# A decoder layer on one core: convolution taps of token tiles 3 and 4 issued behind the second output projection, with a pause, and one norm's rows in other buffers

## The chip, the cores and the metric

One NeuronCore of one Trainium2 chip runs the whole layer as one program. The metric is the device time of one execution in microseconds (us). TensorE (PE) multiplies, VectorE (DVE) and ScalarE (ACT) do the elementwise work, GpSimd (POOL) helps a little, and SyncE (SP) issues most DMAs. Each engine takes its own instructions in the order in which they stand in the program.

## The reference, cut to what matters

```python
hn = rms_norm(h, mix_pre_g); proj = hn @ w_in              # q, k, v and the GLU input u
attn_out = sliding_window_attention(q, k, v, ...)          # window 128, 8 heads
conv_out = conformer_conv(u, ...)                          # GLU, depthwise conv of width 31, LayerNorm, swish, pointwise
mixed = concatenate([attn_out, conv_out]) @ w_out
h = h + rms_norm(mixed, mix_post_g)
hn = rms_norm(h, ffn_pre_g)
ff = (silu(hn @ w_gate) * (hn @ w_up)) @ w_down            # 1024 -> 2816 -> 1024
h = h + rms_norm(ff, ffn_post_g)
```

There are 2048 tokens of width 1024, in float32. Every product is made of three matmuls on a high and a low part of both operands, so each weight and each activation is split first: ACT makes the high part, DVE subtracts it and so makes the low part.

## The kernel before, in words

The 2048 tokens stand in four tiles of 512, numbered 0 to 3 in the code (tile "3 and 4" of the change's name are 2 and 3, "tile 2" is 1). A letter and a number name a stage in every tile's name: A0 to A3 are the input projections, B0 to B3 attention, C0 to C3 the convolution, J0 the joining of two weights, W0 to W3 the output projection with its two norms, H0 and H2 the operands of the feed-forward part for the tile pairs (0, 1) and (2, 3), F0 and F2 its gate and up products for these pairs, G0 and G2 its down products.

A main chain of generators runs in this order: A0 to A3, W1, the first products of F0 (`stage_pre`, 40 products of 12 matmuls with the operands B11 and B21 of tile 0), the rest of F0 (`stage_p1`, whose products need sums over both tiles, made by `stage_h_sums`, called S0), G0, then F2 and G2. Beside it run "lanes". After each step of the main chain each lane is given credit in proportion to the step's length and to its own rate, and issues work until the credit is used (`Lane.pump`). A lane whose `hold()` is true issues nothing. A scheduler then places the instructions of each engine by priority; the lane `lc` has a lag of 100, so that its work stands behind what the main chain issues about then.

`lc` holds the convolution taps: T0, T1 for tiles 0 and 1, T2 for tiles 2 and 3 together. T2 has four channel blocks. For each, `conv_in` loads 527 KB into g2, the first tap is a TENSOR_SCALAR, and 30 taps follow, each a SCALAR_TENSOR_TENSOR of 128x1024 on DVE (line 622 through the recorder on line 85). Then y2 is stored to y_scr. g2 and y2 have one buffer each, so the next block's load and first tap follow that store. T2 runs at rate RC2 = 0.35, and from the third last weight block of F0 at RC3 = 0.9. From the end of W1's main part on, `lc.hold` keeps the taps back until S0 is done.

W1 accumulates into four `mid` tiles. Its second part, `norm_w`, runs in the lane `lh` as N1: it squares the rows (ACT, line 857), takes a first reciprocal root, scales, adds the residual rows of x (loaded by line 870 and 876), stores h, squares again (line 879), takes a second reciprocal root of 12 small DVE instructions (sm@W), scales the four tiles (line 886, ACT) and stores them to hn_scr. The residual rows of its second row block load into two buffers of the tag `mtag`. For W1 that is "at", which has two buffers and is also where attention puts its outputs until they are stored to mixT.

S0 then loads hn_scr back by columns (line 900), turns the blocks on PE (line 922) and makes, for each of four k, five sums on DVE and four splits (ACT and DVE each) in the buffers "chl", of which there are five. F0's second part uses the same five for the loads of its weights' lower halves and for their sums S1 to S4 (`loads`, `sums`), and splits them three products ahead (`split`).

W2, W3, then H2's first half and N3 (the norm of W3) stand in the lane `lw` and run beside G0. W2 and W3 may start only when T2 is done (`since(lc, "T2", CS)`).

Of the kernel before, what the change touches and what calls it, by code (L numbers as in the profile page):

```python
# [37 lines left out]
def layer_kernel(ctx, tc, x, xT, cols, rows, sinks, relb, onehot, w_in, w_four, w_pw, w_out, w_gate, w_up, w_down, out):  # L38
# [16 lines left out]
    def t_(tag, shape, dt=F32):  # L55
        return sb.tile(list(shape), dt, tag=tag, name=nm(tag), bufs=BUFS[tag])

    def f4(tag, shape=(P, D)):
        return t_(tag, shape)

    def f2(tag, shape=(P, T)):
        return t_(tag, shape)

    def hl(tag):
        return t_(tag, (P, 2, T), F32R)

    def sm(n, dt=F32):
        kind = "A" if lab[0][0] == "G" else lab[0][0]
        return sb.tile([P, 8], dt, tag="sm" + kind, name=nm("sm"), bufs={"C": 8, "W": 4}.get(kind, 16))[:, 0:n]

    def bank(tag, bufs):
        return ps.tile([P, T], F32, tag=tag, name=nm(tag), bufs=bufs)

    mm = lambda: bank("mm", 4)
# [178 lines left out]
    y_scr = dr.tile([4, P, S], F32, name="y_scr")  # L253
    qs = {}
    started = set()

    def load_x(t):
        lab[0] = f"A{t}"
        xs = []
        for i in range(4):  # L260
            xt = f4("x", (P, 2, T))
            nc.sync.dma_start(xt, xT[2 * i : 2 * i + 2, :, t * T : (t + 1) * T].rearrange("c p t -> p c t"))
            xs.append(xt)
        started.add(f"x{t}")
        return [xs]
# [368 lines left out]
    def stage_tail(t, sink=None):  # L634
        L = f"C{t}"
        lab[0] = L
        yt = t_("yt", (P, 4, 4 * P))
        ycs = []
        turn = turner(yt, ycs)
        for c in range(4):  # L640
            lab[0] = L
            y = f2("fc")
            nc.sync.dma_start(y, y_scr[c, :, t * T : (t + 1) * T])
            ycs.append(y)
            turn(c)
            yield 0.5
        yield from conv_tail(t, yt, sink)
# [34 lines left out]
    def spare_tile():  # L682
        if not spare:
            spare.append(t_("mb", (P, 2, T)))
        return spare[0]
# [89 lines left out]
    def load_gb(row):  # L775
        gb = []
        for n in range(2):
            t = f2("gb")
            nc.sync.dma_start(t, rows[row, n * T : (n + 1) * T].partition_broadcast(P))
            gb.append(t)  # L780
        return gb
# [6 lines left out]
    def stage_w(w, spill, G, atag, htag, mtag, bank_of, norm=None):  # L788
        L = f"W{w}"
        lab[0] = L  # L790
        acc = [f4(atag) for _ in range(4)]

        def operand(m):
            a = hl(htag)
            act(a[:, 0], m, AF.Copy)
            vtt(a[:, 1], m, a[:, 0].bitcast(F32), ALU.subtract)
            return [a]

        def acts(gi, ms=None):
            return [operand(m) for m in ms or load(gi)]  # L800

        conv = []
        tail = stage_tail(w, lambda v: conv.append(operand(v))) if w > 1 else ()
        for y in tail:
            if y == YL2:
                break
            yield y
        lab[0] = L

        stage = spare_tile() if w == 1 else None  # L810

        def load(gi):
            ms = []
            pair_ = stage if w == 1 else t_("chl", (P, 2, T)) if w else t_("wx", (P, 2, T)) if gi == 0 else None
            for c in range(G * gi, G * gi + G):
                ms.append(pair_[:, c % 2] if pair_ is not None else f2(mtag))
                nc.sync.dma_start(ms[-1], mixT[c, :, w * T : (w + 1) * T])
            return ms

        first = load(0)  # L820
        gb = load_gb(0) if w > 1 else None
        if w != 1:
            yield 5.0 if w == 0 else 8.0
            lab[0] = L
        nxt = acts(0, first)
        for gi in range(KC // G):
            if w > 1 and G * gi == 4:
                yield from tail
                lab[0] = L
            aa = nxt if w < 2 or G * gi < 4 else conv[G * gi - 4 : G * gi - 4 + G]  # L830
            for n in range(2):
                lab[0] = L
                more = gi + 1 < KC // G and (w < 2 or G * gi + G < 4)
                if n == 0 and more:
                    if w < 2 and G * gi + G == 4:
                        ld.until(f"C{w}")
                        lab[0] = L
                    rows_next = load(gi + 1)
                if n == 1 and more:
                    nxt = acts(gi + 1, rows_next)  # L840
                src = w_out[2 * gi : 2 * gi + 2] if gi < 2 else w_join[2 * gi - 4 : 2 * gi - 2]
                ws = weight(src[:, :, n * T : (n + 1) * T].rearrange("c p t -> p c t"),
                            lo_out[n, 2 * gi : 2 * gi + 2], w > 0, on_pool=False)
                yield from block_half(acc, list(zip(aa, ws)), n, gi == 0, L, bank_of)
        last = norm_w(w, spill, acc, mtag, gb)
        if norm:
            norm(last)
        else:
            yield from last

    def norm_w(w, spill, acc, mtag, gb):
        L = f"W{w}"
        lab[0] = L
        gb = gb or load_gb(0)
        ssq = sm(4)
        for s in range(4):
            act(junk, acc[s], AF.Square, accum_out=ssq[:, s : s + 1])
            yield 0.5
            lab[0] = L
        r = rsqrt(ssq, 4, D, False)  # L860
        yield 3
        lab[0] = L
        ssq2 = sm(4)
        for s in range(4):
            lab[0] = L
            post_scale(acc[s], gb, r[:, s : s + 1])
            r0 = w * T + s * P
            if s == (2 if mtag == "fa" else 0):
                xt = f4("wx")
                nc.sync.dma_start(xt, x[r0 : r0 + P])  # L870
                vtt(acc[s], xt, acc[s], ALU.add)
            else:
                for n in range(2):
                    cs = slice(n * T, (n + 1) * T)
                    xt = f2(mtag if s == 1 or w > 1 else "fa")
                    nc.sync.dma_start(xt, x[r0 : r0 + P, cs])
                    vtt(acc[s][:, cs], xt, acc[s][:, cs], ALU.add)
            nc.sync.dma_start(h_scr[r0 : r0 + P], acc[s])
            act(junk, acc[s], AF.Square, accum_out=ssq2[:, s : s + 1])
            yield 5.0  # L880
        lab[0] = L
        r2 = rsqrt(ssq2, 4, D, False)
        yield 3
        lab[0] = L
        for s in range(4):
            act(acc[s], acc[s], AF.Copy, scale=r2[:, s : s + 1])
        if spill:
            yield 2.0
            lab[0] = L
            for s in range(4):  # L890
                r0 = w * T + s * P
                nc.sync.dma_start(hn_scr[r0 : r0 + P], acc[s])
        yield 0.1
        hns[w] = acc
# [301 lines left out]
    def stage_tsums(td):  # L1196
        L = "G0"
        for pr in range(NF // 2):
            lab[0] = L
            wx = f4("wx", (P, 2, T))  # L1200
            b = [wx[:, 0], wx[:, 1], f2("fc"), f2("fc")]
            for i, (f, n) in enumerate(((0, 0), (0, 1), (1, 0), (1, 1))):
                tied(nc.sync.dma_start(b[i], w_down[2 * pr + f, :, n * T : (n + 1) * T]))
            yield 5
            b11, b12, b21, b22 = b
            for to, o, p_, q_ in ((0, b11, b12, b11), (2, b12, b22, b12), (1, b22, b22, b11), (3, b21, b21, b22)):
                lab[0] = L
                vtt(o, p_, q_, ALU.subtract)
                nc.sync.dma_start(td[to, pr], o)
                yield 1  # L1210
# [244 lines left out]
    RC0, RC1, RC2, RC3, RW0, RW, RB, LC = 0.7, 1.1, 0.35, 0.9, 1.7, 1.25, 0.8, 100  # L1455
# [13 lines left out]
    PRE_S0, PRE_S2 = 22, 16  # L1469
# [5 lines left out]
    lc = Lane(RC0, LC)  # L1475
    lw = Lane(RW0, 0)
    lf = Lane(1.2, 0)
    lh = Lane(1.2, 0)
# [7 lines left out]
    def run(gen):  # L1486
        for c in gen:
            clk[0] += c
            for lane in lanes:
                lane.pump(c)  # L1490
# [62 lines left out]
    ws, ops = (0, 1), {}  # L1553
    for n, off in (("B11", 0), ("B21", 4)):
        lh.add(n + ".0", stage_h_plain(ws, ops, n, off), lambda: since(lw, "W0", NH))
    run(stage_w(1, True, 2, "mid", "hl", "at", mm, norm=lambda g: lh.add("N1", g)))
    lc.hold = lambda: "S0" not in lh.done
    lh.add("S0", stage_h_sums(ws, ops), lambda: f"P0.{PRE_S0}" in started and "B3" in lb.done)
    run(stage_pre(ws, ops, mids[0], keeps[0]))
    lt.add("TS", stage_tsums(td))  # L1560
    run(stage_p1(ws, ops, mids[0], keeps[0]))
    lt.until("TS")
    ws, ops = (2, 3), {}
# [76 lines left out]
```

## Time and profile before

| | us |
|---|---|
| three runs | 1906.05, 1906.81, 1908.97 |
| median | 1906.81 |
| profiled execution, span from first to last instruction | 1907.9 |

The profiled execution lies within the three runs, 1.1 us above their median. Its span is what all windows and waits below are counted in, from 0 at the first instruction.

F0's first product starts at 517.84 us, the first product on S0's operands at 639.50 us, F2's first product at 1265.49 us. A matmul's record has a modelled end and overlaps the next one, so how fast PE goes is read from the distance between starts. A row of the list of waits gives who waited, for whom, the total, the count and the longest. A row of the timeline gives start, length, engine, line, operation, written and read tiles, size and count, and in brackets the engine's idle time before it with what ended it.

### The profile page before, as it was taken

To read this page: it belongs to the slowest core of one execution; us is meant where nothing else is said; L and a number is where in the kernel's file an instruction comes from. 1 tells how busy PE (TensorE), PEld (TensorE's weight loads), DVE (VectorE), ACT (ScalarE), POOL (GpSimd) and SP (SyncE) were. 2 spreads that over 40 slices of the span, in tenths; PEclk is the share of its full clock that TensorE was granted. 3 is DMA by queue.
4 is the path that set the end of the run, shared out by engine and by line. 5 is a ranking of instruction groups with operands and counts; after the bars stand their busy time and mean duration, and the time that the engine had idled before them with its cause. 6 is when DMAs were issued, how large, how long until landed. Compare 5 with 4: busy or idle time off the path is not lost.

```text
span 1907.9 us, 26569 instructions
## 1 busy us (share of the span) xinstructions
PE 1889.1 (99%) x8714; PEld 1530.1 (80%) x8714; DVE 1490.7 (78%) x2721; ACT 970.6 (51%) x1912; POOL 179.2 (9%) x196
## 2 busy tenths in 40 slices
PE   9999999999999999999999999999999999999998
PEld 8777777777777888888888878788888888888886
DVE  6999999987966999999996765887567674455558
ACT  5356445566667433433445574685443433345452
POOL 2010001110000000000000000010033233211002
PEclk9999999999999999999999999999999999999999
DMA  9887746679688677877776596798554443375663
GB/s 353 300 281 238 248 160 207 230 228 318 218 274 276 232 234 232 293 261 243 244 268 195 196 326 212 259 333 307 166 176 156 160 138 127 116 258 187 206 220 133
DMA packets 226491, 439.29 MB, mean 230 GB/s; under 512 B 22536, under 2 KB 48560, under 8 KB 226352
## 3 DMA queue, kind: packets, MB, share of 16 engines
q1 hardware_dynamic: 207344, 411.37, 64.8%
q10 hardware_dynamic: 17088, 19.93, 2.9%
q0 software_dynamic: 1920, 6.29, 0.9%
q8 instruction: 68, 1.11, 0.2%
q14 instruction: 71, 0.58, 0.1%
HBM read 318.48 MB, written 119.02 MB: 229 GB/s over the span
## 4 chain that ended last, share of the span: by engine, by line
PE 78%; DVE 9%; DMA 8%; ACT 3%; issue 2%; SPq 0%; ACTq 0%; DVEq 0%; POOL 0%; POOLq 0%
PE mm@F L108 34%; PE mm@G L108 16%; PE mm@A L108 14%; PE tr@W L108 5%; PE mm@W L108 3%; PE tr@B L108 2%; PE ct@J L108 1%; DVE w@F L85 1%; DVE mid@W L85 1%; DMA hl@A<-x 1%; DVE sm@G L85 1%; DVE y2@C L85 1%; DMA chl@H<-hT 1%; DVE hl@G L85 1%; DMA chl@F<-w_gate 1%
## 5 line engine op out<-in xcount | busy, mean ns | idle before, releaser
L108 PE MATMUL mm@F<-hl@H,w@F 128*128 128x512 f32 x1056 | 255.8, 391 | 1.8 <-ACT mm@F L1058 1.6
L108 PEld LDWEIGHTS mm@F<-hl@H,w@F 128*128 128x128 f32 x1056 | 197.7, 188 | 44.8 <-ACT mm@F L1058 2.8
L108 PE MATMUL mm@G<-hl@G,hl@G 128*128 128x512 f32 x924 | 226.1, 393 | 2.3 <-ACT hl@G L904 1.5
L904 ACT ACTIVATE w@F<-chl@F 128x512 fp32r<-128x512 f32 x220 | 136.5, 626 | 170.2 <-PE mm@F L108 158.7
L108 PEld LDWEIGHTS mm@G<-hl@G,hl@G 128*128 128x128 f32 x924 | 171.5, 188 | 39.7 <-ACT hl@G L904 2.2
L108 PE MATMUL mm@G<-w@G,hl@G 128*128 128x512 f32 x876 | 199.8, 389 | 0.6 <-DVE w@G L85 0.6
L108 PEld LDWEIGHTS mm@G<-w@G,hl@G 128*128 128x128 f32 x876 | 164.3, 188 | 35.2 <-DVE w@G L85 1.0
L108 PE MATMUL mm@A<-hl@A,w@A 128*128 128x512 f32 x792 | 192.2, 394 | 0.0
L108 PEld LDWEIGHTS mm@A<-hl@A,w@A 128*128 128x128 f32 x792 | 146.8, 188 | 32.5 <-issue 1.7
L85 DVE TENSOR_TENSOR w@F<-chl@F,w@F 128x512 fp32r<-128x512 f32 x198 | 148.1, 753 | 25.5 <-ACT w@F L904 25.0
L85 DVE SCALAR_TENSOR_TENSOR y2@C<-g2@C,colt,y2@C 128x1024 f32<-128x1024 f32 x120 | 154.0, 1283 | 0.2
L108 PE MATMUL mm@F<-mid@H,w@F 128*128 128x512 f32 x528 | 130.6, 390 | 1.0 <-DVE w@F L85 0.9
L108 PE MATMUL mm@F<-ql@H,w@F 128*128 128x512 f32 x528 | 129.7, 390 | 0.2
L108 PE MATMUL mm@F<-p@H,w@F 128*128 128x512 f32 x528 | 129.1, 389 | 0.0
L108 PE MATMUL mm@F<-x@H,w@F 128*128 128x512 f32 x528 | 127.8, 390 | 0.0
L108 PEld LDWEIGHTS mm@F<-mid@H,w@F 128*128 128x128 f32 x528 | 98.8, 188 | 22.2 <-DVE w@F L85 1.3
L108 PEld LDWEIGHTS mm@F<-ql@H,w@F 128*128 128x128 f32 x528 | 98.7, 188 | 21.3 <-DVE w@F L85 0.6
L108 PEld LDWEIGHTS mm@F<-x@H,w@F 128*128 128x128 f32 x528 | 98.7, 188 | 21.3 <-issue 0.8
L108 PEld LDWEIGHTS mm@F<-p@H,w@F 128*128 128x128 f32 x528 | 99.1, 188 | 20.6
L133 ACT ACTIVATE w@A<-raw@A 128x512 fp32r<-128x512 f32 x100 | 60.9, 625 | 80.2 <-PE mm@A L108 46.3
L85 DVE TENSOR_TENSOR w@G<-raw@G,w@G 128x512 fp32r<-128x512 f32 x72 | 50.2, 698 | 64.2 <-ACT w@G L904 63.4
L108 PE MATMUL mm@W<-w@W,hl@W 128*128 128x512 f32 x384 | 97.1, 399 | 0.8 <-DVE x@W L85 0.4
(322 smaller groups left out, 3363.9 us busy)
## 6 DMA issues: line engine op xcount, KB each, us to landing
mids<-fa@F SPq DMA_DIRECT2D x154, 256.0 KB, 3.3
raw@A<-w_in SPq DMA_DIRECT2D x50, 512.0 KB, 4.9
w@A<-lo_in SPq DMA_DIRECT2D x84, 256.0 KB, 4.0
fa@G<-mids SPq DMA_DIRECT2D x74, 256.0 KB, 4.7
fc@G<-mids SPq DMA_DIRECT2D x72, 256.0 KB, 3.5
w@W<-lo_out SPq DMA_DIRECT2D x48, 256.0 KB, 4.8
chl@F<-w_gate SPq DMA_DIRECT2D x22, 512.0 KB, 4.4
raw@F<-w_gate SPq DMA_DIRECT2D x22, 512.0 KB, 4.2
```

What stands on the lines that cost most here:

```text
L85: r = op(*args, **kw)
L108: r = nc.tensor.matmul(*args, **kw)
L133: act(w[:, 0], raw, AF.Copy)
L904: act(w[:, 0], x, AF.Copy)
```

## The change

```diff
@@ -253,6 +253,7 @@
     started = set()
+    flags = set()
@@ -877,10 +878,13 @@
             act(junk, acc[s], AF.Square, accum_out=ssq2[:, s : s + 1])
+            if s == 2:
+                flags.add("root")
             yield 5.0
         lab[0] = L
         r2 = rsqrt(ssq2, 4, D, False)
         yield 3
+        flags.discard("root")
         lab[0] = L
@@ -1553,11 +1557,13 @@
-    run(stage_w(1, True, 2, "mid", "hl", "at", mm, norm=lambda g: lh.add("N1", g)))
-    lc.hold = lambda: "S0" not in lh.done
+    run(stage_w(1, True, 2, "mid", "hl", "fc", mm, norm=lambda g: lh.add("N1", g)))
+    lc.rates["T2"] = RC3
+    lc.hold = lambda: "root" in flags or f"P0.{PRE_S0}" in started and "S0" not in lh.done
     lh.add("S0", stage_h_sums(ws, ops), lambda: f"P0.{PRE_S0}" in started and "B3" in lb.done)
     run(stage_pre(ws, ops, mids[0], keeps[0]))
     lt.add("TS", stage_tsums(td))
+    lc.rates["T2"] = RC2
     run(stage_p1(ws, ops, mids[0], keeps[0]))
```

The taps of T2 are no longer held from W1's main part on: they run at rate 0.9 in `stage_pre`, are held while N1 is at its second root, and are held again from the 23rd product of `stage_pre` (PRE_S0 = 22) until S0 is done. In `stage_p1` the rate is 0.35 again. The two residual row loads of N1 go to "fc" buffers, which the convolution's tail used before. No instruction is added or removed. What moves is shown at three places, the third on two engines.

**DVE at the second root of N1.** sm@W1 are the root's small instructions, w@F0 the low parts of F0's weights, y2@C2 the taps. Before:

```order
L85 TENSOR_TENSOR mid@W1_787_4738<-at@W1_980_5673,mid@W1_787_4738 128x512
L85 TENSOR_TENSOR w@F0_1028_5984<-raw@F0_1025_5950,w@F0_1028_5984 128x512
L85 TENSOR_TENSOR w@F0_1033_6008<-raw@F0_1029_5987,w@F0_1033_6008 128x512
L85 TENSOR_SCALAR sm@W1_998_5780<-sm@W1_963_5591 128x4
L85 TENSOR_SCALAR sm@W1_999_5781<-sm@W1_998_5780 128x4
L85 TENSOR_SCALAR sm@W1_999_5781<-sm@W1_999_5781 128x4
L85 TENSOR_TENSOR sm@W1_1000_5782<-sm@W1_999_5781 128x4
```

In the changed program:

```order
L85 TENSOR_TENSOR w@F0_1013_5880<-raw@F0_1005_5830,w@F0_1013_5880 128x512
L85 TENSOR_SCALAR y2@C2_958_5570<-g2@C2_957_5568,colt_73 128x1024
L85 TENSOR_SCALAR sm@W1_1000_5791<-sm@W1_965_5597 128x4
L85 SCALAR_TENSOR_TENSOR y2@C2_958_5570<-g2@C2_957_5568,colt_73,y2@C2_958_5570 128x1024
L85 TENSOR_SCALAR sm@W1_1001_5792<-sm@W1_1000_5791 128x4
L85 TENSOR_TENSOR w@F0_1016_5902<-raw@F0_1014_5883,w@F0_1016_5902 128x512
L85 SCALAR_TENSOR_TENSOR y2@C2_958_5570<-g2@C2_957_5568,colt_73,y2@C2_958_5570 128x1024
L85 TENSOR_SCALAR sm@W1_1001_5792<-sm@W1_1001_5792 128x4
L85 TENSOR_TENSOR w@F0_1017_5921<-raw@F0_1014_5883,w@F0_1017_5921 128x512
```

Before, the root starts behind the 21st w@F0 and its 12 instructions end behind the 23rd; now it starts behind the 14th and ends behind the 21st, with 11 full taps among its instructions.

**DVE where F0's second part begins.** chl@H0, ql@H0 and p@H0 belong to the last k of S0, the TENSOR_TENSOR chl@F0<-chl@F0 without raw is the sum S1 of a weight block, w@F0<-chl@F0 the splits that PE needs. Before, around the split w@F0_1173 of the second block:

```order
L85 TENSOR_TENSOR w@F0_1168_6677<-chl@F0_1153_6627,w@F0_1168_6677 128x512
L85 SCALAR_TENSOR_TENSOR y2@C2_1141_6548<-g2@C2_1140_6546,colt_73,y2@C2_1141_6548 128x1024
L85 TENSOR_TENSOR fa@F0_1151_6607<-fa@F0_1151_6607,mm@F0_1149_6590 128x512
L85 TENSOR_TENSOR chl@F0_1191_6815<-chl@F0_1180_6766 128x512
L85 TENSOR_TENSOR w@F0_1173_6705<-chl@F0_1170_6694,w@F0_1173_6705 128x512
```

In the changed program, from the end of S0 on:

```order
L85 SCALAR_TENSOR_TENSOR y2@C2_958_5570<-g2@C2_957_5568,colt_73,y2@C2_958_5570 128x1024
L85 TENSOR_TENSOR chl@F0_1156_6673<-chl@F0_1155_6671 128x512
L85 TENSOR_TENSOR chl@H0_1125_6485<-chl@H0_1119_6468,chl@H0_1125_6485 128x512
L85 TENSOR_TENSOR ql@H0_1137_6542<-chl@H0_1125_6485,ql@H0_1137_6542 128x512
L85 TENSOR_TENSOR fa@F0_1141_6566<-fa@F0_1141_6566,mm@F0_1135_6537 128x512
L85 TENSOR_TENSOR p@H0_1138_6545<-chl@H0_1124_6484,p@H0_1138_6545 128x512
L85 TENSOR_TENSOR chl@F0_1156_6673<-chl@F0_1156_6673,raw@F0_1154_6669 128x512
L85 TENSOR_TENSOR chl@F0_1157_6676<-raw@F0_1154_6669,chl@F0_1155_6671 128x512
L85 TENSOR_TENSOR w@F0_1158_6679<-chl@F0_1156_6673,w@F0_1158_6679 128x512
L85 TENSOR_TENSOR mid@H0_1142_6568<-chl@H0_1125_6485,mid@H0_1142_6568 128x512
L85 TENSOR_TENSOR chl@F0_1157_6676<-raw@F0_1154_6669,chl@F0_1156_6673 128x512
L85 TENSOR_SCALAR y2@C2_1049_6128<-g2@C2_1048_6126,colt_73 128x1024
```

Before, the sum of the third block (chl@F0_1191) stands directly ahead of the split w@F0_1173. In the changed program the splits of the first block stand among the last rows of S0 instead of behind them, a new channel block's first tap (y2@C2_1049) follows, and the third block's sum has gone behind the split that it preceded. By the first split of F0's second part 61 taps have been issued instead of 31; by G0's first split 124, which is all, instead of 100.

**PE at the end of G0.** tr@H2 are the turned blocks of N3's rows, the last operands of F2, mm@F2 its first products, mm@G0 the last ones of G0. Before:

```order
L108 MATMUL mm@G0_1547_9291<-hl@G0_2089_12171,hl@G0_2090_12174 128x512
L108 MATMUL mm@F2_2106_12277<-ql@H2_1930_11256,w@F2_2101_12262 128x512 x3
L108 MATMUL mm@F2_2106_12277<-ql@H2_1937_11283,w@F2_2101_12262 128x512 x3
L108 MATMUL mm@F2_2106_12277<-ql@H2_1941_11302,w@F2_2101_12262 128x512 x3
L108 MATMUL mm@F2_2106_12277<-ql@H2_1951_11340,w@F2_2101_12262 128x512 x3
L922 MATMUL tr@H2_2185_12716<-ident_68,fc@H2_2184_12714 128x128 x4
L922 MATMUL tr@H2_2187_12723<-ident_68,at@H2_2186_12721 128x128 x4
```

In the changed program:

```order
L108 MATMUL mm@G0_1546_9290<-hl@G0_2056_11962,hl@G0_2057_11965 128x512
L926 MATMUL tr@H2_2185_12716<-ident_68,fc@H2_2184_12714 128x128 x4
L108 MATMUL mm@G0_1547_9291<-hl@G0_2043_11875,hl@G0_2044_11878 128x512 x3
L108 MATMUL mm@G0_1547_9291<-hl@G0_2047_11898,hl@G0_2048_11901 128x512 x3
L108 MATMUL mm@G0_1547_9291<-hl@G0_2056_11962,hl@G0_2057_11965 128x512
L926 MATMUL tr@H2_2187_12723<-ident_68,at@H2_2186_12721 128x128 x4
```

Of the turned blocks of N3's rows the first now stand behind 813 and 820 of G0's 924 matmuls instead of behind all of them. W3's last matmul followed 660 of them before and follows 521 now.

**SP late in G0.** fa@G0 and mb@G0 are the loads of G0's products, hn_scr the four stores of the tiles that N3 has scaled on ACT. Before:

```order
L1262 DMA fa@G0_2078_12106<-mids0_4730 128x512
L1266 DMA mb@G0_2079_12108<-w_down 128x512 x2
L1262 DMA fa@G0_2082_12129<-mids0_4730 128x512
L1262 DMA fa@G0_2085_12149<-mids0_4730 128x512
L1266 DMA mb@G0_2086_12151<-w_down 128x512
L892 DMA hn_scr_125<-mid@W3_1762_10404 128x1024
L892 DMA hn_scr_125<-mid@W3_1763_10405 128x1024
```

In the changed program:

```order
L1266 DMA fa@G0_2038_11850<-mids0_4730 128x512
L896 DMA hn_scr_125<-mid@W3_1762_10404 128x1024
L896 DMA hn_scr_125<-mid@W3_1763_10405 128x1024
L896 DMA hn_scr_125<-mid@W3_1764_10406 128x1024
L896 DMA hn_scr_125<-mid@W3_1765_10407 128x1024
L1266 DMA fa@G0_2042_11873<-mids0_4730 128x512
L1270 DMA mb@G0_2039_11852<-w_down 128x512 x2
L1266 DMA fa@G0_2045_11893<-mids0_4730 128x512
L1270 DMA mb@G0_2046_11895<-w_down 128x512 x2
L1266 DMA fa@G0_2055_11960<-mids0_4730 128x512
L904 DMA fc@H2_2184_12714<-hn_scr_125 128x4x128
L904 DMA at@H2_2186_12721<-hn_scr_125 128x4x128
```

The four stores stood behind the loads of all of G0's products; now fa@G0_2042, mb@G0_2039 and what follows stand behind them, and these belong to the products at G0's 793rd to 829th matmul. On ACT the four scales stood behind the splits hl@G0_2081 (877th matmul) and stand behind hl@G0_2030 (745th) now.

## The prediction

> **What bounds the kernel now.** I read the page first, then the list of waits of PE from the start of F0's second part on, then the chain.
>
> ```profile
> span 1907.9 us, 26569 instructions
> PE 1889.1 (99%) x8714; PEld 1530.1 (80%) x8714; DVE 1490.7 (78%) x2721; ACT 970.6 (51%) x1912; POOL 179.2 (9%) x196
> ```
>
> PE is busy for 99% of the span, DVE for 78%. The change neither adds nor removes an instruction, so it can gain only what PE waits for, and lose only by new waits. The waits of PE between 565 us and the end, which holds everything that the change moves:
>
> ```profile
> PE mm@F L108 <- ACT mm@F L1058: 1.6, 1, 1.6
> PE mm@G L108 <- ACT hl@G L904: 1.5, 2, 0.8
> PE mm@F L108 <- DVE w@F L85: 0.9, 1, 0.9
> PE tr@H L922 <- DMA at@H<-hn_scr: 0.7, 1, 0.7
> PE mm@G L108 <- DVE p@G L1297: 0.6, 1, 0.6
> PE mm@G L108 <- DVE w@G L85: 0.6, 1, 0.6
> PE mm@F L108 <- DVE gb@F L85: 0.5, 1, 0.5
> PE mm@F L108 <- ACT gb@F L1159: 0.2, 1, 0.2
> ```
>
> All but the wait for w@G, which falls in G2, stand between the root of N1 and the first products of F2: 1.6 + 1.5 + 0.9 + 0.7 + 0.6 + 0.5 + 0.2 = **6.0 us**. That is the ceiling of the gain. From there on the chain says that PE has nothing to wait for:
>
> ```profile
> 1225.59 5.72 DMA mb@G<-w_down
> ...
> 1256.45 6.18 DMA hn_scr<-mid@W
> 1263.07 6.64 DMA at@H<-hn_scr
> ...
> 1295.02 391.70 PE mm@F L108 x1728
> ```
>
> **The taps and their room on DVE.** The 120 full taps and four first ones, by stretch, and the busy time of DVE in three stretches:
>
> ```profile
> L85 DVE SCALAR_TENSOR_TENSOR y2@C<-g2@C,colt,y2@C 128x1024 f32<-128x1024 f32 x120 | 154.0, 1283 | 0.2
> 482.00:543.00 61.00, 10.41 (x8) 1.00 0.63 215
> 543.00:634.00 91.00, 0.00 (x0) 1.00 0.83 279
> 634.00:951.00 317.00, 88.15 (x70) 1.00 0.75 248
> 951.00:1012.00 61.00, 29.43 (x23) 1.00 0.79 269
> ```
>
> ```profile
> 551.00:594.00 43.00, 14.96 (x32) 1.00 0.86 296
> 594.00:634.00 40.00, 36.75 (x59) 1.00 0.77 252
> 640.00:700.00 60.00, 54.18 (x78) 1.00 0.69 230
> ```
>
> The first four of these rows' windows count taps alone (busy us, then their number), the last three all of DVE. No tap runs from 543 to 634 us, and the last 23 of them run in G0. The order has 61 taps instead of 31 ahead of the first split of F0's second part, so 30 move into that gap. A tap takes 1283 ns by its group, and two that follow each other start about 1.20 us apart (the tap below at 646.34 is followed by the next start at 647.54). So the 30 need 30 x 1.20 = **36.0 us**. The room is 43.0 - 14.96 = 28.0 and 40.0 - 36.75 = 3.3, so **31.3 us**. At least 4.7 us do not fit and stand ahead of the work that follows. Between 640 and 700 another 60.0 - 54.18 = 5.8 us are idle, which can take that backlog up, though only once PE's first operands are past it.
>
> **Step 1, the root of N1.** The rows that carry it:
>
> ```profile
> 558.52 0.42 SPq L876 DMA_DIRECT2D at@W<-x  x1
> ```
>
> ```profile
> 570.77 0.69 DVE L85 TENSOR_TENSOR w@F<-raw@F,w@F 128x512 fp32r<-128x512 f32 x1 [1.35 <-ACT w@F L904]
> 575.47 0.36 DVE L85 SCALAR_TENSOR_TENSOR sm@W<-sm@W,sm@W 128x4 f32<-128x4 f32 x2
> ```
>
> ```profile
> 575.87 4.27 ACT L886 ACTIVATE mid@W<-mid@W,sm@W 128x1024 f32<-128x1024 f32 x4 [2.05 <-DVE sm@W L85]
> ```
>
> The root's last small instructions end at 575.83. ACT has idled 2.05 us for them, then scales four tiles in 4.27 us, and everything of ACT stands behind that; this is where PE waits 1.6 us for ACT's mm@F. The residual row was issued only at 558.52, behind an attention output that held its "at" buffer; from "fc" it comes earlier, and since SP takes its queue in order the weight loads behind it come earlier too. Against that, 11 full taps now stand among the root's instructions. Their end stands behind the 21st split instead of the 23rd; the 21st is the row at 570.77 us. So the root can end at 571.5 at best, and at 575.83 + 2 x 1.28 = 578.4 if two taps push it beyond its old place. I take 574.5, with two taps and the root's remainder behind the 21st split, because the splits ahead of it are paced by ACT and not by DVE (its 1.35 us of idle). ACT starts its scales 1.3 us earlier. **-1.3 us** of the 1.6, bounds -1.6 and +2.6. The pause by the flag keeps the lane silent at the root only where the lane is asked; the order shows what it left standing.
>
> **Step 2, the first product of F0's second part.**
>
> ```profile
> 630.67 0.69 DVE L85 TENSOR_TENSOR w@F<-chl@F,w@F 128x512 fp32r<-128x512 f32 x1
> 638.54 0.68 DVE L85 TENSOR_TENSOR w@F<-chl@F,w@F 128x512 fp32r<-128x512 f32 x1
> 645.13 0.69 DVE L85 TENSOR_TENSOR chl@F<-chl@F 128x512 f32<-128x512 f32 x1 [2.31 <-DMA chl@F<-w_gate]
> 646.34 1.28 DVE L85 SCALAR_TENSOR_TENSOR y2@C<-g2@C,colt,y2@C 128x1024 f32<-128x1024 f32 x1
> ```
>
> ```profile
> 639.50 1.52 PE L108 MATMUL mm@F<-mid@H,w@F 128*128 128x512 f32 x6
> 646.48 1.20 PE L108 MATMUL mm@F<-mid@H,w@F 128*128 128x512 f32 x4 [0.92 <-DVE w@F L85]
> ```
>
> The first split ended at 630.67 + 0.69 = 631.36, and PE took it at 639.50: 8.1 us ahead. A backlog of 4.7 us brings it to 636.1. Some idle time stays unused, because a row that waits for a load holds the taps behind it (1.35 and 2.31 us in the rows above): I add the largest of them, and get 638.4, **1.1 us ahead of PE**. PE's one wait here, 0.9 us at 646.48, came from a split that stood directly behind the third block's sum, which itself waited 2.31 us for its load. In the changed order that sum has gone behind the split. So the wait goes unless the backlog is there instead, and I take half of it: **-0.4 us**, bounds -0.9 and +1.2 (one more hole of 2.31 us, less the 1.1 ahead).
>
> One row speaks against the change here: the tap at 646.34 has its operands long before, and yet DVE idles 2.31 us ahead of the sum at 645.13 that stands before it. By the Trainium skill, Perfetto Trace Analysis, section "Tensor Engine Instruction (MATMUL, LD_WEIGHTS)", "ACT/DVE/GPSIMD are strict FIFO", so a ready tap can't fill such a hole, nor a split pass a tap; the trace agrees with its 2.31 us. Without that rule the 36.0 us of taps would fill the 31.3 us of room at no cost to a split, and step 2 would be -0.9; with it the first rival below follows.
>
> **Step 3, the rest of F0's second part.** Its other waits are 0.5 and 0.2 us. 24 taps fewer stand in G0, but F0's own second part holds about as many as before, in other places, and starts with a backlog. The buffers "chl" come free with the splits, so a late split delays the next load. I take **+0.5 us**, bounds -0.7 (both waits go) and +4 (the backlog of 4.7 us reaches PE once, in the place of these 0.7).
>
> **Step 4, G0 and the start of F2.** 24 taps x 1.20 = 29 us leave DVE here; it was not what PE waited for, but two of its splits were. W3's last matmul stands 660 - 521 = 139 matmuls earlier, and N3 follows it.
>
> ```profile
> 1216.44 15.68 PE L108 MATMUL mm@G<-hl@G,hl@G 128*128 128x512 f32 x68
> 1232.96 7.41 PE L108 MATMUL mm@G<-hl@G,hl@G 128*128 128x512 f32 x28 [0.84 <-ACT hl@G L904]
> ```
>
> ```profile
> 1216.95 0.69 DVE L85 TENSOR_TENSOR hl@G<-fa@G,hl@G 128x512 fp32r<-128x512 f32 x1
> 1269.85 0.63 PE L922 MATMUL tr@H<-ident,at@H 128*128 128x128 f32 x4 [0.72 <-DMA at@H<-hn_scr]
> ```
>
> ```profile
> 1249.48 4.27 ACT L886 ACTIVATE mid@W<-mid@W,sm@W 128x1024 f32<-128x1024 f32 x4
> ```
>
> In the first row 68 matmuls take 15.68 us, 0.23 each. It begins with the 725th, so the 745th started 20 x 0.23 = 4.6 us later, near 1221.0, and its split (1216.95 + 0.69) was ready 3.4 us ahead. N3's four scales now stand behind that split. Before, from the scales' start at 1249.48 to the issue of the last store at 1256.45 were 7.0 us, and to the turned block at 1269.85 were 20.4. A load of mb@G issued at 1225.59 fed the product that PE waited for until 1232.96: 7.4 us. In the changed order the loads of the 793rd matmul's product follow the stores on SP: 7.0 + 1.5 (issues of some 0.4 us each) + 7.4 - 3.4 = 12.5 us behind the 745th matmul, and due at 48 x 0.23 + 0.6 (four turned blocks between, by the row at 1269.85) = 11.6. PE waits **0.9 us** there. The turned blocks can start at 20.4 - 3.4 = 17.0 and are due at 75 x 0.23 + 0.6 = 17.9: their 0.7 us goes, with 0.9 to spare. So 2.8 us of waits in G0 and at F2 (1.5 + 0.6 + 0.7) become 0.9 and 1.3 (the hl@G wait of 0.7 and the p@G one of 0.6 belong to the norm before and are left as they are): **-0.6 us**, bounds -2.8 (all go) and +5 (the split is no more ahead than PE's 0.84 us wait showed, so both the stores and the blocks come 3 to 4 us later, with the other loads behind them).
>
> **The sum.** -1.3 - 0.4 + 0.5 - 0.6 = -1.8 us. The profiled execution's span of 1907.9 lies 1.1 above the median, and would become 1906.1; the same difference from the median of 1906.81 gives **1905.0 us**.
>
> **The rivals.**
> - *DVE's backlog reaches PE (slower).* A channel block ends close to 634 us, as one did near 546:
>
> ```profile
> 545.78 0.43 SPq L631 DMA_DIRECT2D y_scr<-y2@C  x1
> 546.26 0.50 SPq L605 DMA_DIRECT2D g2@C<-glu_scr  x1
> ```
>
> ```profile
> g2@C<-glu_scr SPq DMA_DIRECT2D x4, 527.0 KB, 5.5
> ```
>
>   The next block's first tap stands right behind the first splits and waits for the store and 5.5 us of load. Where DVE reaches it before the load is in, the second split is late by up to 5.5 - 1.1 = 4.4, and the blocks after it by some 1.6 more (a guess from the +0.5 to +4 of step 3) while "chl" refills: +6, so 1912.8 us. It decides from 1.1 us of further delay of DVE on. For it speaks the sum of step 2, against it that the backlog itself gives the load time to arrive.
> - *SP's order in G0 (slower).* N3's stores wait on SP ahead of the loads of five products; if the splits run only as far ahead as where PE waited, step 4's upper bound falls due: +5, so 1911.8. Against it: DVE has 29 us less to do there.
> - *Most waits go (faster).* The root ends early, splits stay ahead, G0 has an idle DVE and the spill is in time: the ceiling of 6.0, so 1900.8. For it speaks that each wait is under 1.7 us and that every one stands beside something the change moves away.
> - *It does little.* The root's order is earlier by seven splits, but the 11 taps eat that, and the wait stays where it was: 1906.8.
>
> **How the numbers follow.** Forecast 0.30 (1903 to 1908), most waits go 0.27, DVE's backlog 0.19, SP's order 0.14, little 0.10. A difference of 0.2%, 3.8 us, is about what a measurement of this kernel can tell from no change; that is below 1903.0 or above 1910.6. Faster 0.27, within 0.40 (forecast and little), slower 0.33 (the two slow ones). The range of 1900.0 to 1913.0 holds the ceiling's end and most of both slow cases; the forecast's own is 1903 to 1908.
>
> **What would show it.** Step 1: the root's last sm@W near 574.5, and ACT's scales at 574.6. Step 2: DVE's busy time between 551 and 634 up by some 31 of its 31.3 idle us, and the first w@F<-chl@F ending within a microsecond of PE's first product on mid@H; a wait for w@F after it, and one of a first tap for g2, is the first rival. Step 4: waits for hl@G behind N3's stores and none for at@H. A new wait of several us, or a span more than 4 us off with none, would make the forecast wrong.

## The result, and the profile after

| us | median | runs |
|---|---|---|
| before | 1906.81 | 1905.57 to 1908.97 (5) |
| changed | 1913.48 | 1912.00 to 1915.00 (5) |

The ratio is 1.0034, with a 95% interval of 1.0021 to 1.0047: the change makes the kernel **6.7 us slower**. An execution's time is longer than its span: the profiled execution of the changed kernel took 1913.48 us with a span of 1911.5, so 2.0 us lie around the span. In the kernel before it is 1.7 to 1.8 us (1907.25 and 1905.5 in its second profile below). By that the profiled execution of before, with its span of 1907.9, took about 1909.6 and not 1907.9. It lay 2.8 us above its median, and above the highest of the five runs.

The head of the page of the changed kernel:

```profile
span 1911.5 us, 26546 instructions
PE 1889.9 (99%) x8714; PEld 1532.4 (80%) x8714; DVE 1489.4 (78%) x2721; ACT 972.1 (51%) x1912; POOL 181.9 (10%) x196
```

PE has the same work; the span has grown by waits. PE's waits of the changed kernel, as before who waited, for whom, total, count and longest:

```profile
PE tr@H L926 <- issue: 3.0, 1, 3.0
PE mm@G L108 <- ACT mm@G L1341: 1.4, 1, 1.4
...
PE mm@F L108 <- ACT at@F L1166: 0.7, 1, 0.7
...
PE mm@F L108 <- ACT mm@F L1062: 0.6, 1, 0.6
...
PE mm@G L108 <- DVE hl@G L85: 0.5, 1, 0.5
PE mm@F L108 <- ACT gb@F L1163: 0.5, 2, 0.2
```

The waits for w@F (0.9) and at@H (0.7) are gone. So is the wait of 1.6 for ACT's mm@F, which stood at 581 us behind N1's scales: the wait of 0.6 that bears the same name is another one, 30 us ahead of the scales. There ACT had stood 3.55 us before the load of a weight:

```profile
542.93 0.63 ACT L908 ACTIVATE w@F<-raw@F 128x512 fp32r<-128x512 f32 x1 [3.55 <-DMA raw@F<-w_gate]
544.59 3.04 PE L108 MATMUL mm@F<-hl@H,w@F 128*128 128x512 f32 x12 [0.62 <-ACT mm@F L1062]
```

The new long wait is one of 3.0 for a turned block tr@H, longer than any before. Taps and DVE's busy time in the windows of the prediction:

```profile
543.00:634.00 91.00, 40.46 (x32) 1.00 0.77 270
634.00:951.00 317.00, 79.35 (x63) 1.00 0.74 250
951.00:1012.00 61.00, 0.00 (x0) 1.00 0.79 275
```

```profile
551.00:594.00 43.00, 40.23 (x55) 1.00 0.77 269
594.00:634.00 40.00, 39.68 (x56) 1.00 0.72 246
640.00:700.00 60.00, 59.05 (x87) 1.00 0.77 266
```

The first three rows count taps alone: 32 now run where none ran (the first of them, at 544.43, is one that ran at 541.32 before), none is left in G0. DVE has 3.1 us of idle left between 551 and 634 where it had 31.3, and 0.9 between 640 and 700 where it had 5.8.

To see where the time goes I split each profiled execution at three starts that can be read from PE's timeline: F0's first product, the first product on mid@H (F0's second part), and F2's first product.

| profile | to F0 | F0's first part | second part and G0 | F2 to the end |
|---|---|---|---|---|
| before | 517.8 | 121.7 | 626.0 | 642.4 |
| before, second profile | 518.1 | 121.4 | 624.0 | 642.0 |
| changed | 520.6 | 120.8 | 626.1 | 644.0 |
| changed, second profile | 521.0 | 121.1 | 626.5 | 645.1 |
| without the root's pause (same program) | 518.7 | 120.9 | 627.2 | 644.6 |

Sixteen matmuls of turned blocks, some 0.11 us each and 1.8 together, have moved from F2 into G0. With that taken into account the third column is between 1.7 us better than the first profile of before and 1.4 us worse than the second, and F2 has lost 644.6 - 642.2 + 1.8 = 4 us. F0's first part has gained 0.6. The stretch ahead of F0 is taken up in the experiments.

PE at the start of F2, before and then in the changed kernel (start, length, line, tiles, count, idle before):

```profile
1265.49 3.04 PE L108 MATMUL mm@F<-ql@H,w@F 128*128 128x512 f32 x12
1270.23 2.99 PE L108 MATMUL mm@F<-ql@H,w@F 128*128 128x512 f32 x12
```

```profile
1267.49 2.88 PE L108 MATMUL mm@F<-ql@H,w@F 128*128 128x512 f32 x12
1273.33 1.09 PE L926 MATMUL tr@H<-ident,fc@H 128*128 128x128 f32 x4 [2.95 <-issue]
1274.07 4.06 PE L108 MATMUL mm@F<-ql@H,w@F 128*128 128x512 f32 x12
```

The load of the rows fc@H had been issued by SP near 1233.5, some 40 us earlier. What PE waits for is seen on DVE:

```profile
1268.64 0.75 DVE L85 SCALAR_TENSOR_TENSOR p@G<-p@G,sm@G,wx@G 128x512 f32<-128x512 f32 x1 [4.31 <-DMA wx@G<-h_scr]
1269.31 0.75 DVE L85 SCALAR_TENSOR_TENSOR x@G<-x@G,sm@G,wx@G 128x512 f32<-128x512 f32 x1
1269.97 1.28 DVE L1301 COPY p@G<-mm@G 128x512 f32<-128x512 f32 x2
1271.17 1.40 DVE L85 SCALAR_TENSOR_TENSOR chl@H<-tr@H,colt,chl@H 128x512 f32<-128x512 f32 x2
1272.48 0.74 DVE L85 SCALAR_TENSOR_TENSOR p@H<-tr@H,colt,p@H 128x512 fp32r<-128x512 f32 x1
```

The turned blocks go to three banks of PSUM, the memory that PE writes its results to (the tag "tr", line 75). N3's first block, turned at 1240.38, was read at 1242.25. The next three, turned from 1242.43 to 1255 us, took the three banks, and the fifth can start when DVE has read the one that it replaces. Those readers stand behind G0's output norm on DVE. That norm waited 4.31 us for a row of wx@G, of which there is one buffer, so that its next load is issued only when the norm has read the last one (SP issued it at 1264.35, the norm's last reading had ended at 1264.32). The last reader of the second block ends at 1272.48 + 0.74 = 1273.22, and PE starts at 1273.33. In the two other executions of this program listed above PE starts 0.10 us behind the end of the same reader.

In the kernel before, DVE reads N3's first turned block at 1271.83, about as late as the second one here, but there PE turns it only at 1268.49:

```profile
1267.95 0.75 DVE L85 SCALAR_TENSOR_TENSOR p@G<-p@G,sm@G,wx@G 128x512 f32<-128x512 f32 x1 [0.65 <-POOL sm@G L162]
1271.83 0.75 DVE L85 SCALAR_TENSOR_TENSOR chl@H<-tr@H,colt,chl@H 128x512 f32<-128x512 f32 x1
```

### The profile page after: what moved, and what is told of

Its sections match the earlier page's. It is cut to its first block, busy times and chain, and to the rows that moved or that the text cites. A ratio compares the mean times of both kernels' runs of the same rounds, so it can differ in the third digit from the quotient of the medians.

```text
span 1911.5 us, 26546 instructions
## 1 busy us (share of the span) xinstructions
PE 1889.9 (99%) x8714; PEld 1532.4 (80%) x8714; DVE 1489.4 (78%) x2721; ACT 972.1 (51%) x1912; POOL 181.9 (10%) x196
## 4 chain that ended last, share of the span: by engine, by line
PE 70%; DVE 4%; DMA 1%; issue 1%; ACT 1%; DVEq 0%; ACTq 0%; SPq 0%
PE mm@F L108 43%; PE mm@G L108 19%; PE tr@W L108 4%; PE mm@W L108 2%; DVE sm@G L85 1%; DVE mid@W L85 1%; PE tr@H L926 1%; DMA raw@W<-w_out 0%; PE tr@B L108 0%; DMA at@W<-x 0%; DVE x@G L85 0%; DVE hl@G L85 0%; DVE x@W L85 0%; DVE fa@G L85 0%; DMA raw@F<-w_gate 0%
```

## The experiments

Theory **T** said that the loss is this wait and what comes with it, caused by N3's turned blocks standing earlier. Rival **W** said that it is lost ahead of F0, in W1, where the other buffers give another order: the first profile began F0 2.76 us later than before.

**The kernel before, a second profile** (no edit).

> The kernel before once more, unchanged, for a second profiled execution beside the first (span 1907.9 us, which with the 2.0 us around it lies some 3 us above the median of the timed runs). Theory T (turned blocks: the change loses at the start of F2, where N3's turned blocks, standing earlier, use up three PSUM banks whose readers are late; 3.0 us) and theory W (the change loses before F0, in the output projection W1, where the other buffers give another order; F0 began 2.75 us later) both say: F0's first product near 517.8, no wait for a turned block over 1 us at the start of F2. If F0 begins 1 us or more from 517.8, that part of the difference between the two profiles is chance.

Measured 1907.25 us; F0 at 518.08, PE's longest wait for tr@H 0.5. The two profiles of before agree to 0.3 us up to F0's second part. There the first one had 2 us more, the wait for w@F of 0.9 among them, which the second doesn't have. So one of the waits that the prediction counted as a gain is there in only some executions.

**The other buffers alone**, in the kernel before.

```diff
-    run(stage_w(1, True, 2, "mid", "hl", "at", mm, norm=lambda g: lh.add("N1", g)))
+    run(stage_w(1, True, 2, "mid", "hl", "fc", mm, norm=lambda g: lh.add("N1", g)))
```

> The kernel before with the other buffers for N1's rows alone; the taps are held as before, G0 and F2 stand in the same order as before. Theory W: F0 begins 1.4 to 2.8 us later than before and the time is 1908 to 1910. Theory T: no wait at the start of F2 beyond 0.7 us, the time within 1 us of before or a little faster for the earlier root (1905.5 to 1907.5).

Measured 1905.86 us, ratio to before 0.9995 (0.9986 to 1.0004), F0 at 517.82: against W. And yet the root has moved far. ACT's scales in this kernel, and PE's only wait for ACT's mm@F:

```profile
555.96 4.28 ACT L886 ACTIVATE mid@W<-mid@W,sm@W 128x1024 f32<-128x1024 f32 x4 [0.90 <-DVE sm@W L85]
```

```profile
542.21 3.02 PE L108 MATMUL mm@F<-hl@H,w@F 128*128 128x512 f32 x12 [1.02 <-ACT mm@F L1058]
```

The rows come earlier, and the scales start at 555.96 instead of 575.87, 20 us sooner. The wait behind them is gone (1.6 and 1.3 us in the two profiles of before), and the other one ahead of them has come, so PE gains 0.3 to 0.5 us in all. The kernel with the old buffers below has no such wait ahead of the root: it comes with the other buffers.

**The taps alone, with the old buffers**, in the changed kernel.

```diff
-    run(stage_w(1, True, 2, "mid", "hl", "fc", mm, norm=lambda g: lh.add("N1", g)))
+    run(stage_w(1, True, 2, "mid", "hl", "at", mm, norm=lambda g: lh.add("N1", g)))
```

> The change without the other buffers: taps go on in F0's first part, with the pause, N1's rows load into the buffers of before. The program is that of before up to F0's first part. Theory T: the wait of some 3 us for a turned block after F2's first 12 matmuls is there, and the time is as slow as the changed kernel's, 1911 to 1914, or slower by the root's later rows. Theory W: F0 begins as before at 517.8, and the time is 1 to 3 us better than the changed kernel's, 1909 to 1912.

Measured 1924.33 us, 1.0090 (1.0075 to 1.0106). T had left room for a later root, but neither theory had this size: the other buffers, worth nothing by themselves, are worth 11 us once the taps go on. The wait for tr@H is there too, with 2.9 us. PE of this kernel at the start of F0's second part, then N1's scales on ACT in this kernel and in the changed one:

```profile
651.53 1.22 PE L108 MATMUL mm@F<-mid@H,w@F 128*128 128x512 f32 x2 [10.70 <-ACT w@F L908]
655.13 1.22 PE L108 MATMUL mm@F<-ql@H,w@F 128*128 128x512 f32 x2 [2.38 <-ACT w@F L908]
```

```profile
595.62 4.28 ACT L890 ACTIVATE mid@W<-mid@W,sm@W 128x1024 f32<-128x1024 f32 x4 [1.33 <-DVE sm@W L85]
```

```profile
574.34 4.28 ACT L890 ACTIVATE mid@W<-mid@W,sm@W 128x1024 f32<-128x1024 f32 x4 [0.26 <-DVE sm@W L85]
```

The root's twelve small instructions take 4.0 us on DVE before (571.81 to 575.83). With taps among them they take from 554.97 to 574.30 in the changed kernel, 19 us, and from 575.31 to 595.6 here: each stands behind a tap. The early rows of the other buffers pay for that and little more. Without them the scales, N1's stores to hn_scr and S0's loads of them are 21 us later than in the changed kernel (the first store is issued at 596.80 instead of 575.78).

**W2 put off**, in the changed kernel.

```diff
+    g0 = clk[0]
-    lw.add("W2", stage_w(2, ...), lambda: since(lc, "T2", CS))
+    lw.add("W2", stage_w(2, ...), lambda: since(lc, "T2", CS) and clk[0] >= g0 + 20)
```

> The changed kernel with W2's start in G0 put off by 20 us of the main chain's steps, so that W3's last matmul follows 652 of G0's (660 before, 521 in the changed kernel) and N3's turned blocks stand again at the end of G0 and in F2. Theory T: the wait of 3.0 us at the start of F2 falls under 1 us and the time falls by 2 to 4 us, to 1909.5 to 1911.5. Theory W: the wait may go, but the time stays within 1 us of 1913.5, since F0 begins as late as in the changed kernel.

Measured 1906.95 us, 0.9999 (0.9990 to 1.0008): all of the loss is gone, more than T expected. The wait at the start of F2 is gone and so is the slow stretch behind it:

```profile
1262.11 3.04 PE L108 MATMUL mm@F<-ql@H,w@F 128*128 128x512 f32 x12
1264.99 0.60 PE L926 MATMUL tr@H<-ident,fc@H 128*128 128x128 f32 x4
1265.34 3.02 PE L108 MATMUL mm@F<-ql@H,w@F 128*128 128x512 f32 x12
```

The split of this profile is 516.9, 121.0, 624.2 and 641.4. Up to G0 its instructions stand exactly as in the changed kernel, so its F0 at 516.9 against 520.6 can't come from the program's order.

**The changed kernel, a second profile** (no edit).

> The changed kernel once more, unchanged. Its first profile began F0 at 520.60, while the kernel with the late W2, whose program is the same up to G0, began it at 516.91: chance, if F0 begins near 518 here. Theory T (all the loss lies in G0 and at the start of F2): time 1912 to 1915 again, the wait of about 3 us for a turned block after F2's first 12 matmuls and the wait of 1.4 us for ACT in G0 are both there again. Theory W (a part is lost before F0): F0 begins at 520 or later again.

Measured 1912.51 us (1908.62 to 1915.73), 1.0027 (1.0017 to 1.0037). The wait for tr@H is 3.2. F0 began at 521.03 this time too, in an execution that was the slowest of its nine.

**N3 alone put off**, in the changed kernel.

```diff
+    g0 = clk[0]
-    lw.add("W3", stage_w(3, ..., norm=lambda g: lw.add("N3", g)), ...)
+    lw.add("W3", stage_w(3, ..., norm=lambda g: lw.add("N3", g, lambda: clk[0] >= g0 + 150)), ...)
```

> The changed kernel with N3 alone put off (W2 and W3 stand as early as in the changed kernel, W3's last matmul behind 521 of G0's), so that N3's turned blocks stand where they stood before, two of them behind F2's first 12 matmuls. Theory T in its narrow form (the early turned blocks are the cause): the 3.0 us wait falls under 1 us and the time to 1907 to 1909.5. Rival E (it is W2's and W3's own early work beside G0's first half that costs): the time stays at 1911 or more although the wait at F2 is gone.

Measured 1907.83 us, 1.0006 (0.9998 to 1.0015), its split 518.8, 120.9, 624.0 and 642.2. The longest wait for tr@H is 0.3. W2 and W3 stand as early as in the changed kernel, so E falls. N3's own work on ACT, DVE and SP has moved too, so this run alone doesn't tell the turned blocks from the rest of N3; the next one does.

**A second buffer for the output norm's rows**, in the changed kernel.

```diff
-            ht = f4("wx" if L == "G0" else "mid")
+            nth[0] += L == "G0"
+            ht = f4(("y2" if nth[0] % 2 else "wx") if L == "G0" else "mid")
```

> The changed kernel with two buffers instead of one for the residual rows of G0's output norm (every other row load goes to the buffer of the taps' sums, idle by then). Theory T says that DVE reads the turned blocks late because it stands 4.3 us before a row load of that norm: with two buffers this wait falls to under 2 us, the 3.0 us wait for a turned block falls to under 1.5 and the time by 1.5 to 3 us, to 1910.5 to 1912. If the bank is not what PE waits for, the wait at F2 and the time (1913 to 1914) stay.

Measured 1908.07 us, 1.0008 (1.0000 to 1.0017), 5.4 less than the changed kernel's first median and more than expected. DVE of this kernel where it stood 4.31 us before, and PE:

```profile
1260.93 0.75 DVE L85 SCALAR_TENSOR_TENSOR p@G<-p@G,sm@G,y2@G 128x512 f32<-128x512 f32 x1
1264.98 1.29 DVE L1303 COPY p@G<-mm@G 128x512 f32<-128x512 f32 x2 [0.83 <-PE mm@G L108]
1266.42 1.41 DVE L85 SCALAR_TENSOR_TENSOR chl@H<-tr@H,colt,chl@H 128x512 f32<-128x512 f32 x2
```

```profile
1265.73 3.02 PE L108 MATMUL mm@F<-ql@H,w@F 128*128 128x512 f32 x12
1268.59 0.63 PE L927 MATMUL tr@H<-ident,fc@H 128*128 128x128 f32 x4
1268.97 2.98 PE L108 MATMUL mm@F<-ql@H,w@F 128*128 128x512 f32 x12
```

Nothing of the turned blocks' places was changed here, only the row load that DVE waited for. Its wait went. The readers of the turned blocks start 0.7 us behind F2's first product (1266.42 and 1265.73) where they started 3.7 behind it (1271.17 and 1267.49), and PE goes on. So the early blocks cost F2 nothing where their readers come in time. The split is 517.6, 120.8, 627.4 and 640.2. With the 1.8 us of the moved blocks, F2 is level with before.

**The taps with the old buffers and W2 put off** (both edits from above).

> The taps go on without the other buffers (1924.3 us), with W2's start put off by 20 us as in the kernel with the late W2. Theory T: 6 us less, as there (1913.5 to 1906.95), so 1917 to 1919: the two losses, 13 us of waits for ACT's w@F at F0's second part from the old buffers and some 6 from the end of G0, add up. If they are one and the same, it stays near 1924 or falls to 1909.

Measured 1921.38 us, 1.0079 (1.0066 to 1.0092): 2.9 us less, not 6. The 13.4 us of waits at F0's second part stay, and the wait of 2.9 for a turned block is gone, so they are two losses. F2 takes 641.3 us instead of 644.1, although it has taken back the 1.8 us of turned blocks, so it gains 4.6, near the 4 us of the changed kernel. Why the median gains only 2.9 is not shown: the profiled execution of the taps alone was the slowest of its four (1929.88 us, the others 1923.26 to 1924.90), so the two profiles can't be compared as a whole.

**The pause around the root taken out**, in the changed kernel.

```diff
-    lc.hold = lambda: "root" in flags or f"P0.{PRE_S0}" in started and "S0" not in lh.done
+    lc.hold = lambda: f"P0.{PRE_S0}" in started and "S0" not in lh.done
```

> The changed kernel without the pause around N1's second root. It issues the same instructions in the same order on all five engines, since the scheduler's places did not depend on the pause, so it is a third execution of the changed kernel. Every theory: 1912 to 1915. Theory T: the wait of 3 us behind F2's first 12 matmuls is there. Theory W (a loss before F0): F0 begins at 520 or later for the third time; by chance it begins between 516.9 and 518.8, as in four kernels that are the same up to G0.

Measured 1911.75 us, 1.0027 (1.0017 to 1.0038), with the 3 us wait (3.2) again. F0 began at 518.74. The changed kernel's program thus begins F0 at 520.6, 521.0 and 518.7, the kernels that are the same up to G0 at 516.9 (W2 put off), 518.8 (N3 put off) and 517.6 (second buffer): the program's order doesn't decide it, and W is not borne out. Programs that are the same up to G0 thus differ by up to 4.1 us in where F0 begins. Why the two slowest were both profiles of the same file stays open.

**The old buffers with fewer taps** (the old buffers, and rate 0.6 instead of RC3).

> Taps that go on with the old buffers for N1's rows, as in the run of 1924.3 us, but at rate 0.6 instead of 0.9 in F0's first part, so that 59 taps stand ahead of F0's first split on S0's sums instead of 71 (62 in the changed kernel). Theory B (DVE's backlog: it is the number of taps ahead of the split that decides): the wait of 13 us for w@F at the start of F0's second part falls under 1 us and the time to 1911 to 1914, as the changed kernel. Rival R (the old buffers make the rows, the root and S0 late): 5 us or more of the wait stay, 1917 or more.

Measured 1920.97 us, 1.0074 (1.0060 to 1.0088). R holds: though 59 taps stand ahead, fewer than in the changed kernel, PE still waits 7.4 us there, and the spill's first store is issued at 594.72 instead of 575.78.

```profile
PE mm@F L108 <- ACT w@F L908: 7.4, 2, 4.2
```

```profile
594.00:634.00 40.00, 27.73 (x43) 1.00 0.85 283
```

DVE, whose busy time the second row gives, idles for 12.3 us between 594 and 634 here (0.3 in the changed kernel), so it had room before the late work reached it. With twelve taps fewer the wait went from 13.1 to 7.4, so their number has a part in it; the rest goes with the late root.

**Second buffer without the change** (the kernel before with "fc" and the second row buffer).

> The kernel before with the other buffers for N1's rows and with two buffers for the residual rows of G0's output norm; the taps are held as before. If the waits near the end of G0 and at F2's start (0.7 and 0.2 us in that kernel) are all that the second buffer can take, the time is 1905 to 1906, within 1 us of the other buffers alone (1905.86); were the norm's row loads a wider brake, 1903 to 1904.5.

Measured 1906.08 us, 0.9995 (0.9986 to 1.0003): nothing to take there, as before the readers were not in the way.

**W2 put off and second buffer together** (from the changed kernel).

> The changed kernel with W2 put off by 20 us of the main chain's steps and with two buffers for the output norm's rows. Theory T: both take away the same loss (6.5 and 4.4 us alone), so together they give no more than the larger: 1905.5 to 1907.5. If they were separate losses, 1902 to 1904.

Measured 1907.97 us, 1.0005 (0.9996 to 1.0014). The two don't add up; they take away the same loss. No kernel of these beats the one before beyond its interval.

## Why the prediction was wrong

The time of 1913.48 lies above the range's end of 1913.0, and the sign was the slow rivals'. The other two medians of this program, 1912.51 and 1911.75, lie inside the range, but they too are slower than before, where the forecast was faster. That the first rival's 1912.8 is close is chance, since its wait didn't come. Point by point:

- *The taps and their room*: right. 32 taps ran between 543 and 634, and DVE's idle time between 551 and 634 went from 31.3 to 3.1 us. The order has 62 taps and not 61 ahead of the first split of F0's second part, so 31 moved and not 30, 1.2 us more.
- *Step 1, the root*: right in its direction, and its time by luck. The scales were put at 574.6 and started at 574.34, but in an execution that began F0 2.76 us late: counted from F0's first product they start after 53.7 to 54.1 us in the three profiles of the changed program, where they started after 57.8 and 58.0. So the root came 4 us earlier and not 1.3, and the wait behind it (1.6 and 1.3 in before's two profiles) went whole. In its place the wait ahead of the root came, of 0.6, 1.0 and 0.6, which the step did not have: forecast -1.3, measured -0.7 in all. What was not seen either: the root had 20 us to win from the buffers and the taps took most of them. And the pause, which was taken as working "where the lane is asked", moves no instruction.
- *Step 2, the first split*: right, in the changed kernel:

```profile
638.47 0.71 DVE L85 TENSOR_TENSOR w@F<-chl@F,w@F 128x512 fp32r<-128x512 f32 x1
```

  It ended at 639.18, and PE took it at 641.36 without a wait, 2.2 us later where 1.1 were forecast. The first rival, DVE's backlog, didn't happen: the first tap of the next block waited 0.95 us for g2, not 5.5. In the kernel with the old buffers a backlog, without that load, is a part of the loss. The gain was counted on a wait of 0.9 that the second profile of before doesn't have.
- *Step 3*: right by its waits: 0.7 for ACT's at@F and 0.5 for gb@F stand where 0.7 stood, +0.5 as forecast. That the buffers "chl" bring them is not shown; no experiment looked into them.
- *Step 4, G0 and the start of F2*: **the step that failed**: "their 0.7 us goes, with 0.9 to spare", and -0.6 in all. The turned blocks did come in time:

```profile
1240.38 0.60 PE L926 MATMUL tr@H<-ident,fc@H 128*128 128x128 f32 x4
```

  That row has no wait in it. But the step followed the blocks only as far as PE and did not ask who reads them and what stands ahead of the readers on DVE. From the second block on they stood behind the output norm, as late as before, so that the second block held its bank from 1242.43 to 1273.22, 31 us, two more blocks held the others, and PE waited 2.95 us for one. The waits of the step, 2.8 us before, became 5.2: 2.95, 1.44 for a bank of G0 that ACT had not read yet, 0.5 and 0.3. The second rival named the same stretch with another cause, SP's order: of the 0.9 us forecast behind N3's stores nothing is seen, since from 1200 us on PE waits only for ACT's bank of G0 and for the turned block. The step's upper bound of +5 holds what came, but for the rival's reason and not for this one.
- *The price of the wait* was larger than the wait: about 4 us. PE's clock in six windows of 1 us, changed kernel (window, length, PE busy and count, granted clock, DMA share, GB/s):

```profile
1272.00:1273.00 1.00, 0.00 (x0) 0.97 1.02 274
1273.00:1274.00 1.00, 0.67 (x4) 0.50 0.84 272
1274.00:1275.00 1.00, 1.00 (x4) 0.50 0.96 371
1275.00:1276.00 1.00, 1.00 (x4) 0.50 0.13 49
1276.00:1277.00 1.00, 1.00 (x5) 0.83 0.69 270
1277.00:1278.00 1.00, 1.00 (x6) 1.00 0.41 45
```

  When the wait ends the clock is at 0.50 and stays there for some 3 us, and the next 12 matmuls take 4.06 us where 12 took 2.99 to 3.04 before, 1.0 us more on top of the wait of 2.95.
- *The sum* took a span for a time: the profiled execution of before lay 2.8 us above its median and not 1.1. The forecast of 1905.0 doesn't hang on that, but part of the 6.0 us of waits, the ceiling, was not there to be gained: the second profile of before has 5.0 of them.

Of 6.7 us, F2's 4 are shown by three kernels that take them away in different ways (by 6.5, 5.7 and 5.4 us from 1913.48, and by 3.7 us at least from the lowest median of the changed program, 1911.75). Up to 1.4 us lie between F0's second part and F2, where the wait for ACT's mm@G (1.4, 0.4 and 1.1 in the three profiles) is one that the kernel with the late W2 doesn't have; its cause is not shown. Some 0.3 us lie around the span. The rest lies ahead of F0, where the executions of one program differ by up to 2.3 us, and its cause is not settled.

## What to carry to other kernels

When a producer moves earlier, follow its output to the last reader: if the reader stays where it is on an in-order engine, the buffers between them are held longer, and the producer's engine is the one that waits. Time won for one chain is soon spent where other work is let in among its instructions: twelve instructions of 0.16 us took 19 us among taps of 1.2. And compare spans with spans: one profiled execution may hold waits that the median doesn't.

## What the runs showed of the hardware that was not expected

A wait of PE of 2.95 to 3.2 us lowered its granted clock in all three executions of the changed program: to 0.50 for some 3 us in each (the rows above for the first). Behind the 1.44 us wait at 1204 it stayed at 1.00. The length of one wait doesn't decide it alone: in the kernel with the taps alone two waits of 1.23 and 0.50 us, which ended at 1094.60 and 1096.29, lowered it too (0.50 from 1097 to 1099). In the same kernel the waits of 10.70 and 2.38 us lowered it to the same 0.50, but for longer:

```profile
640.00:652.00 12.00, 1.30 (x5) 0.75 0.18 66
652.00:656.00 4.00, 1.62 (x4) 0.50 0.63 219
656.00:660.00 4.00, 4.00 (x11) 0.55 0.98 354
660.00:670.00 10.00, 10.00 (x45) 1.00 0.49 165
```

In windows of 1 us it is 0.50 from 646 to 659 us, and 1.00 from 660 on; 0.75 and 0.55 are means over a window in which it changes. The Trainium skill, TensorE: Matmul & The Clock Gate, in its Part 1 on the HAM clock gate, tells of a clock that falls to half after an idle window of about 3.4 us and comes back after a busy one. The 0.50 agrees; that a wait of 2.95 us is enough, and two shorter ones close together, is what these runs add.
